# Another use of spare weight buffers, and a fourth seven-product pair in the last gate/up block

## The chip, the cores and the metric

The kernel runs on one core of one Trainium2 chip. The metric is the device time of one execution in microseconds (us). The median of three runs before the change is 1083.32 us (1082.24 to 1083.6).

PE is the matrix engine, DVE the vector engine, ACT the scalar engine, POOL the general-purpose engine, SP the engine that only issues transfers. "DMA" is a transfer between the chip's main memory and its on-chip memory.

## The reference

One decoder layer over 256 tokens with 2048 features, in float32. Cut to what matters here:

```python
u = rmsnorm(h, ln1_w[l])
proj = jnp.einsum('bsd,de->bse', u, w_in[l])
...                                   # recurrent heads and retention heads
y = jnp.concatenate([y_lru, y_ret], axis=-1)
h = h + jnp.einsum('bse,ed->bsd', y, w_out[l])
u = rmsnorm(h, ln2_w[l])
ff = jax.nn.silu(jnp.einsum('bsd,df->bsf', u, w_ffn_gate[l])) * jnp.einsum('bsd,df->bsf', u, w_ffn_up[l])
h = h + jnp.einsum('bsf,fd->bsd', ff, w_ffn_down[l])
return rmsnorm(h, final_norm_w)
```

The gate, up and down products (2048 by 5632, twice, and 5632 by 2048) are the largest part of the work.

## The kernel before, in words

**Precision.** A float32 matrix product is made of three passes in a faster format. Each operand is split into a high part (ACT rounds it, line 123) and a low part (DVE subtracts, line 124). `three` (lines 683 to 685) then issues high x high, high x low, low x high. So every weight tile that arrives must go through ACT and DVE before PE can use it.

**Blocks.** The output projection has two blocks (0, 1), gate/up eleven (2 to 12), down two (13, 14). A block makes two by two output tiles (c11, c12, c21, c22): two groups of 128 tokens by two groups of 512 weight columns. In a gate/up block one column group belongs to gate and the other to up. It sums over pairs of 128 features: eight pairs in blocks 0 to 12, 22 pairs in each block of down. A pair's weights are two raw tiles of 128 x 1024 (512 KB each), which are two column groups for two feature groups.

**Eight or seven products.** A pair is a 2 x 2 by 2 x 2 product of tiles. Done plainly it takes 8 products (`EIGHT`). A summed pair takes 7, by Strassen's method in Winograd's form: sums of the left tiles (s1 to s4) and of the weight tiles (t1 to t4, made by DVE in `add`, line 661) are multiplied in place of some of the tiles. In blocks 1 to 12 the seven products of a summed pair are done in two places. Four products (`share`) go to accumulators in the block *before*, and are combined there at the end of the shares (lines 805 to 811). Three products (`DIRECT`) are added in the block itself. For the share step both raw tiles are loaded, for the direct step the second one once more (class `Direct`, one load).

**Steps.** `SUMMED` names the summed pairs of each block, and `STEPS` the order of its work: p is a plain pair, s a share of the next block's summed pair, d a direct step of this block's, h half of a plain pair. Blocks 4 to 10 have four shares, four directs, and four plain pairs of which two are cut in halves. Block 12, the last of gate/up, shares three pairs for down (`EARLY_DOWN`). The left operands of those pairs (class `Left`: split, and for a summed pair four sums and another split) are made in block 12 too. The first block of down does its 22 pairs in the order `ORDER_DOWN`: 3, 4, 0, 5, 6, 1, 7, 8, 2, 9, and so on. Pairs 0, 1 and 2 are direct steps, 9, 12, 15, 17 and 19 are summed in place.

**Order.** The work is written out as a list of steps (`program`). A loop walks through it and issues the loads of the steps ahead by three raw tiles (`AHEAD`), then the step's products. All transfers of weights are issued by SP (lines 141, 641, 743, 771). A planner with a model of times then orders the instructions of each engine, gives out buffers, and puts in the waits; so the order on an engine is not exactly that of the list. Some work is deferred by a number of steps (`defer`, `tick`).

**Buffers.** Six raw tiles (`rpool`) and four pairs of split tiles (`wpool`). From block 3 on (`swap`) the space of the early stages gives two raw tiles and two pairs of split tiles more (`more`). Before the change a counter of all raw tiles sends every fourth load to an extra raw tile, and another counter every third split to an extra split tile. 60 tiles of 128 x 512 (`act_tile`) hold the activations, the left operands and some sums. `stop_more`, ahead of block 12, ends the use of the extra tiles. `swap_back`, ahead of down, gives their space to the residual rows, which lie in memory since the output projection and come back by POOL's queue (line 1112), and to the weights of the last norm (line 893).

Of the kernel before, what the change touches and what calls it, by code (L numbers as in the profile page):

```python
# [30 lines left out]

SUMMED = ((), (4, 5), (2, 3), (1, 2, 3)) + ((0, 1, 2, 3),) * 8 + ((1, 2, 3),)
SUMMED_OUT, SUMMED_FFN = (4, 5), (0, 1, 2, 3)

PLAIN = ((4, 5, 6, 7, 0, 1, 2, 3),) * 2 + (tuple(range(8)),) * 11
STEPS = ("pppspppspp", "ppspdpsdpp", "pdpsdpspspp", "pspsdpsdpsdp") + ("psdhsdhsdhsdhp",) * 7 + ("psdpsdpsddp", "psdpsdpsdpp")

# [7 lines left out]
def tile_hymba_layer(ctx: ExitStack, tc: tile.TileContext, A: dict, out: bass.AP):  # L45
# [5 lines left out]
    rpool = ctx.enter_context(tc.tile_pool(name="raw", bufs=6))  # L51
# [4 lines left out]
    tpool = early.enter_context(tc.tile_pool(name="tmp", bufs=6))  # L56
    late, resid, more, turn_of = [], [xpool], [], [0, 0]
    extra = ExitStack()
# [15 lines left out]
    def split_tiles():  # L74
        turn_of[1] += 1
        pool_ = more[1] if more and turn_of[1] % 3 == 0 else wpool
        return [pool_.tile([P, 1024], F32R, tag=g, name=nm(g)) for g in ("wh", "wl")]

    def raw_tile():
        turn_of[0] += 1  # L80
        pool_ = more[0] if more and turn_of[0] % 4 == 0 else rpool
        return pool_.tile([P, 1024], F32, tag="raw", name=nm("raw"))
# [76 lines left out]
    program = []  # L159
# [297 lines left out]
    half = {}  # L457
# [156 lines left out]
    NB = DFF // 512  # L614
    ff = [None] * (FT // 2)

    class Quad:
# [5 lines left out]
        def __init__(self, src, sums, before=None):  # L623
            self.src, self.sums, self.before = src, sums, before
            self.parts = {}
            self.apart = False

# [11 lines left out]
        def load(self, half):  # L639
            r = raw_tile()  # L640
            nc.sync.dma_start(out=r, in_=self.src[:, half * 1024 : half * 1024 + 1024])
            if half == 0 and self.before:
                self.before()
            if not self.sums:
                self.cut(("b22", "b21") if half else ("b11", "b12"), r)
                return
            if half == 0:
                self.ra = r
                self.parts["b11"] = act_tile("bh", F32R), act_tile("bl", F32R)
                split(*self.parts["b11"], r[:, :512])  # L650
                return
            self.cut(("b22", "b21"), r)
            self.add(r)
            self.cut(("t1", "t3"), self.ra)
            self.cut(("t2", "t4"), r)
# [31 lines left out]
    def block(index, quads, lefts, post, ps, tail, early={}, ordered=False):  # L687
# [39 lines left out]
        for i in range(n):  # L727
            program.append(([quads[i]], step(i)))

        def end():  # L730
# [29 lines left out]
    class Direct(Quad):  # L760
# [8 lines left out]
        def load(self, half):  # L769
            r = raw_tile()  # L770
            nc.sync.dma_start(out=r, in_=self.src[:, 1024:2048])
            self.cut(("b22", "b21"), r)
            self.parts["t4"] = self.shared.parts["t4"]
# [12 lines left out]
    class Block:  # L786
# [45 lines left out]
        def put(self, after):  # L832
            plain = [i for i in PLAIN[self.index] if i not in self.summed]
            for k, kind in enumerate(self.steps):
                if kind == "p":
                    i, n = plain.pop(0), len(plain)
                    quad = Quad(self.src(i), False)
                    run = lambda i=i, quad=quad, k=k, n=n: self.plain(i, quad, k == 0, n == 0)
                elif kind == "h":
# [266 lines left out]
    def swap_back():  # L1106
# [6 lines left out]
        load_fw()  # L1113

    blocks = [Block(d, lambda i, d=d: A["w_out"][8 * d + i], y, out_post(d), STEPS[d], SUMMED[d]) for d in range(2)]
    blocks += [
# [4 lines left out]
    for b, after in zip(blocks, blocks[1:] + [down]):  # L1121
        if b.index == 3:
            program.append(([], swap))
        if b.index == NB + 1:
            program.append(([], stop_more))
        b.put(after)
    program.append(([], swap_back))

# [119 lines left out]
```

## Time and profile before

| what | value |
|---|---|
| median of three runs | 1083.32 us |
| the profiled execution, its own time | 1082.46 us |
| its span, first to last instruction | 1080.7 us |
| granted clock of the matrix engine, mean | 0.998 |
| PE busy, share of the span | 1070.2 us, 99% |
| DVE busy | 964.1 us, 89% |
| ACT busy | 664.5 us, 61% |
| raw tiles loaded for gate/up, 512 KB each | 216 |
| raw tiles loaded for down, 512 KB each | 91 |

The page splits the span into 40 slices and gives the busy share of each engine in tenths. The chain that ended last is followed from the last instruction back to what released it. Groups of instructions carry the line of the kernel, the engine, the tile written and the tiles read (`c<-wl,ah` is a matmul into an accumulator c from a low weight part and a high activation part), the count, the busy time and the mean. In views in order of time the first number is the start and the second the duration, both in us.

### The profile page before, as it was taken

To read this page: it belongs to the slowest core of one execution; us is meant where nothing else is said; L and a number is where in the kernel's file an instruction comes from. 1 tells how busy PE (TensorE), PEld (TensorE's weight loads), DVE (VectorE), ACT (ScalarE), POOL (GpSimd) and SP (SyncE) were. 2 spreads that over 40 slices of the span, in tenths; PEclk is the share of its full clock that TensorE was granted. 3 is DMA by queue.
4 is the path that set the end of the run, shared out by engine and by line. 5 is a ranking of instruction groups with operands and counts; after the bars stand their busy time and mean duration, and the time that the engine had idled before them with its cause. 6 is when DMAs were issued, how large, how long until landed. Compare 5 with 4: busy or idle time off the path is not lost.

```text
span 1080.7 us, 14590 instructions
## 1 busy us (share of the span) xinstructions
PE 1070.2 (99%) x5089; PEld 897.7 (83%) x5089; DVE 964.1 (89%) x1399; ACT 664.5 (61%) x947; POOL 57.2 (5%) x73
## 2 busy tenths in 40 slices
PE   9999999999999999999999999999999999999997
PEld 7888888888888888888888888888888888888886
DVE  7889789988878889989999999999999889997886
ACT  7666644468756676656656565665656656654563
POOL 0602230000000000000000000000002000000001
PEclk9999999999999999999999999999999999999999
DMA  9965475554556588677776777777767856474662
GB/s 325 336 213 171 159 254 166 183 176 158 192 195 234 183 304 273 231 235 256 257 270 228 251 260 242 263 269 232 258 234 270 289 181 214 162 245 159 214 212 101
DMA packets 71386, 244.62 MB, mean 226 GB/s; under 512 B 8208, under 2 KB 8592, under 8 KB 71312
## 3 DMA queue, kind: packets, MB, share of 16 engines
q1 hardware_dynamic: 68400, 236.34, 64.6%
q0 software_dynamic: 1472, 4.72, 1.3%
q10 hardware_dynamic: 1440, 2.62, 0.6%
q8 instruction: 40, 0.66, 0.2%
q14 instruction: 34, 0.28, 0.1%
HBM read 239.46 MB, written 4.19 MB: 225 GB/s over the span
## 4 chain that ended last, share of the span: by engine, by line
PE 98%; DVE 1%; DMA 1%; POOL 0%; SPq 0%; ACT 0%; issue 0%; POOLq 0%; ACTq 0%
PE c L685 22%; PE c L683 22%; PE c L684 22%; PE fm L194 11%; PE fm L196 5%; PE tm L174 3%; PE tm L175 3%; PE tm L176 3%; PE p L683 1%; PE p L685 1%; PE p L684 1%; PE ft L865 1%; DMA x<-in_x 1%; PE ht L588 0%; PE sc L492 0%; DVE wl L124 0%
## 5 line engine op out<-in xcount | busy, mean ns | idle before, releaser
L123 ACT CAST wh<-raw 128x1024 fp32r<-128x1024 f32 (+1 forms) x498 | 462.9, 959 | 323.8 <-PE c L685 130.8
L124 DVE TENSOR_TENSOR wl<-raw,wh 128x1024 fp32r<-128x1024 f32 (+1 forms) x498 | 542.2, 1115 | 72.5 <-ACT wh L123 71.2
L684 PE MATMUL c<-wl,ah 128*128 128x512 f32 x826 | 322.7, 391 | 0.0
L685 PE MATMUL c<-wh,al 128*128 128x512 f32 x826 | 321.8, 390 | 0.0
L683 PE MATMUL c<-wh,ah 128*128 128x512 f32 x826 | 280.3, 391 | 0.0
L683 PEld LDWEIGHTS c<-wh,ah 128*128 128x128 f32 x826 | 155.1, 188 | 32.0 <-ACT wh L123 0.3
L685 PEld LDWEIGHTS c<-wh,al 128*128 128x128 f32 x826 | 155.2, 188 | 31.8
L684 PEld LDWEIGHTS c<-wl,ah 128*128 128x128 f32 x826 | 155.2, 188 | 31.6
L194 PE MATMUL fm<-u,wh 128*128 128x512 f32 x512 | 161.4, 396 | 0.0
L196 PEld LDWEIGHTS fm<-u,wl 128*128 128x128 f32 x512 | 96.1, 188 | 22.4
L196 PE MATMUL fm<-u,wl 128*128 128x256 f32 x512 | 101.2, 279 | 0.0
L661 DVE TENSOR_TENSOR raw<-raw,raw 128x512 f32<-128x512 f32 x114 | 78.4, 689 | 2.0
L661 DVE TENSOR_TENSOR raw<-raw 128x512 f32<-128x512 f32 x114 | 78.3, 688 | 1.4
L194 PEld LDWEIGHTS fm<-u,wh 128*128 128x128 f32 x512 | 78.4, 189 | 0.3
L684 PE MATMUL c<-wl,sh 128*128 128x512 f32 x192 | 74.3, 390 | 0.0
L685 PE MATMUL c<-wh,sl 128*128 128x512 f32 x192 | 73.7, 390 | 0.0
L683 PE MATMUL c<-wh,sh 128*128 128x512 f32 x192 | 67.3, 391 | 0.3 <-ACT sh L123 0.3
L176 PE MATMUL tm<-wh,u 128*128 128x512 f32 x128 | 48.7, 391 | 0.0
L175 PE MATMUL tm<-wl,u 128*128 128x512 f32 x128 | 48.7, 393 | 0.0
L174 PE MATMUL tm<-wh,u 128*128 128x512 f32 x128 | 46.9, 394 | 1.4 <-ACT u L298 1.4
L683 PEld LDWEIGHTS c<-wh,sh 128*128 128x128 f32 x192 | 36.1, 188 | 8.1 <-ACT sh L123 0.7
L685 PEld LDWEIGHTS c<-wh,sl 128*128 128x128 f32 x192 | 36.1, 188 | 7.5
(247 smaller groups left out, 1027.4 us busy)
## 6 DMA issues: line engine op xcount, KB each, us to landing
raw<-in_w_gu SPq DMA_DIRECT2D x216, 512.0 KB, 5.3
raw<-in_w_down SPq DMA_DIRECT2D x91, 512.0 KB, 4.6
raw<-in_w_out SPq DMA_DIRECT2D x34, 512.0 KB, 3.7
raw<-in_w_lx SPq DMA_DIRECT2D x16, 512.0 KB, 6.4
raw<-in_w_k SPq DMA_DIRECT2D x16, 512.0 KB, 3.6
raw<-in_w_q SPq DMA_DIRECT2D x16, 512.0 KB, 4.2
raw<-in_w_rg SPq DMA_DIRECT2D x16, 512.0 KB, 3.5
raw<-in_w_lg SPq DMA_DIRECT2D x16, 512.0 KB, 3.5
```

The costliest lines, as they stand in the source:

```text
L123: act.copy(out=dst_h, in_=src)
L124: v.tensor_tensor(out=dst_l, in0=src, in1=dst_h.bitcast(F32), op=ALU.subtract)
L174: pe.matmul(ps, ah, wh, start=first, stop=False)
L175: pe.matmul(ps, ah, wl, start=False, stop=False)
L176: pe.matmul(ps, al, wh, start=False, stop=last)
L194: pe.matmul(ps, wh, hl, start=n + i == 0, stop=False)
L196: pe.matmul(ps[:, :S], wl, hl[:, :S], start=False, stop=n + i == len(order) - 1)
L661: v.tensor_tensor(out=dst, in0=a, in1=b, op=ALU.add)
L683: pe.matmul(p, ah, bh, start=first, stop=False, skip_group_check=onto)
L684: pe.matmul(p, ah, bl, start=False, stop=False, skip_group_check=onto)
L685: pe.matmul(p, al, bh, start=False, stop=last, skip_group_check=onto)
L865: pe.transpose(pt[:, o : o + P], g[:, (2 * b + c) * P : (2 * b + c) * P + P], ident)
```

## The change

- Block 12's summed pairs become (0, 1, 2, 3) instead of (1, 2, 3). So block 11 shares four pairs, with the steps that blocks 4 to 10 have, and block 12 takes the steps that block 11 had.
- The extra raw tiles no longer go to every fourth load. They go to the load of each direct step, and to the second load of a block's last plain pair (`brief`).
- The counter of splits stays (every third).
- `stop_more` moves from the start of block 12 to behind the tenth step of the first block of down (position 9, pair 9). `swap_back`, with the residual rows' return, moves from the start of down to behind its thirteenth step (position 12, pair 12).

```diff
-SUMMED = ((), (4, 5), (2, 3), (1, 2, 3)) + ((0, 1, 2, 3),) * 8 + ((1, 2, 3),)
+SUMMED = ((), (4, 5), (2, 3), (1, 2, 3)) + ((0, 1, 2, 3),) * 9
...
-STEPS = ("pppspppspp", "ppspdpsdpp", "pdpsdpspspp", "pspsdpsdpsdp") + ("psdhsdhsdhsdhp",) * 7 + ("psdpsdpsddp", "psdpsdpsdpp")
+STEPS = ("pppspppspp", "ppspdpsdpp", "pdpsdpspspp", "pspsdpsdpsdp") + ("psdhsdhsdhsdhp",) * 8 + ("psdpsdpsddp",)
...
     def split_tiles():
-        turn_of[1] += 1
-        pool_ = more[1] if more and turn_of[1] % 3 == 0 else wpool
+        turn_of[0] += 1
+        pool_ = more[1] if more and turn_of[0] % 3 == 0 else wpool
...
-    def raw_tile():
-        turn_of[0] += 1
-        pool_ = more[0] if more and turn_of[0] % 4 == 0 else rpool
+    def raw_tile(brief=False):
+        pool_ = more[0] if more and brief else rpool
...
         def load(self, half):
-            r = raw_tile()
+            r = raw_tile(self.brief and half == 1)
...
         for i in range(n):
             program.append(([quads[i]], step(i)))
+            if i in hooks[ordered]:
+                program.append(([], hooks[ordered][i]))
...
     class Direct(Quad):
...
         def load(self, half):
-            r = raw_tile()
+            r = raw_tile(True)
...
                     quad = Quad(self.src(i), False)
+                    quad.brief = n == 0
...
+    hooks = {0: {9: stop_more, 12: swap_back}, 1: {}}
...
         if b.index == 3:
             program.append(([], swap))
-        if b.index == NB + 1:
-            program.append(([], stop_more))
         b.put(after)
-    program.append(([], swap_back))
```

More of the change, by code (lines that the diff above doesn't have):

```diff
@@ L56, in tile_hymba_layer @@
     tpool = early.enter_context(tc.tile_pool(name="tmp", bufs=6))
-    late, resid, more, turn_of = [], [xpool], [], [0, 0]
+    late, resid, more, turn_of = [], [xpool], [], [0]
     extra = ExitStack()
@@ L625, in __init__ @@
             self.parts = {}
-            self.apart = False
+            self.apart = self.brief = False
         def cut(self, names, raw):
```

## The prediction

> **What bounds the kernel now.** I read the page first, then PE's waits, then PE's order of time, then the stretches of the blocks that the change touches.
>
> ```profile
> span 1080.7 us, 14590 instructions
> ...
> PE 1070.2 (99%) x5089; PEld 897.7 (83%) x5089; DVE 964.1 (89%) x1399; ACT 664.5 (61%) x947; POOL 57.2 (5%) x73
> ...
> PEclk9999999999999999999999999999999999999999
> ...
> PE 98%; DVE 1%; DMA 1%; POOL 0%; SPq 0%; ACT 0%; issue 0%; POOLq 0%; ACTq 0%
> ...
> L123 ACT CAST wh<-raw 128x1024 fp32r<-128x1024 f32 (+1 forms) x498 | 462.9, 959 | 323.8 <-PE c L685 130.8
> ```
>
> PE is on 98% of the chain that ended last, at full clock in every slice; DVE is next, busy 89%. A busy PE can still run below its pace, so the next two views matter more. The first is everything that PE waited for, in the whole span (us in total, times, longest); the second is PE's order of time where the last gate/up block begins.
>
> ```profile
> PE tm L174 <- ACT u L298: 1.4, 2, 1.0
> PE warm L116 <- DVE eps_t L109: 1.1, 1, 1.1
> PE c L683 <- ACT sh L123: 0.3, 1, 0.3
> ```
>
> ```profile
> 812.37 0.39 PE L683 MATMUL c<-wh,ah 128*128 128x512 f32 x1
> 812.60 0.39 PE L684 MATMUL c<-wl,ah 128*128 128x512 f32 x1
> 812.82 0.39 PE L685 MATMUL c<-wh,al 128*128 128x512 f32 x1
> 813.05 0.39 PE L683 MATMUL c<-wh,ah 128*128 128x512 f32 x1
> ```
>
> PE waited 2.8 us in all, and none of it in the gate/up blocks from the second on or in down: the two larger waits are at the start, and the third, 0.3 us, is on the path in an output-projection block. Starts follow each other by (813.05 - 812.37) / 3 = **0.227 us** for one matmul of 512 columns. So this kernel is a count of matmuls times 0.227 us over almost its whole length. There is no stall in the changed stretch that more buffers could remove; they can only prevent one.
>
> **The change part by part.**
>
> *The products.* Each product is three matmuls. A plain pair has 8 products (24 matmuls); a summed pair has 4 in the share step and 3 in the direct step (12 + 9 = 21). Pair 0 of the last gate/up block goes from plain to summed. In the block before it, the steps become those of the eight blocks with four shares and four directs: 12 matmuls more there. In the last block a plain pair goes (-24) and a direct step comes (+9). Net 12 - 24 + 9 = **-3 matmuls, 3 x 0.227 = -0.68 us**. The name of the change says four such pairs, but three of them are there already; only one is new.
>
> *What the new pair costs off PE.* One weight tile more is loaded (512 KB), and DVE and ACT split and add more. The prices are DVE's starts in a stretch where it runs without a gap:
>
> ```profile
> 892.52 1.22 DVE L124 TENSOR_TENSOR wl<-raw,wh 128x1024 fp32r<-128x1024 f32 x1
> 893.65 0.68 DVE L124 TENSOR_TENSOR bl<-raw,bh 128x512 fp32r<-128x512 f32 x1
> 894.25 1.22 DVE L124 TENSOR_TENSOR wl<-raw,wh 128x1024 fp32r<-128x1024 f32 x1
> 895.39 0.69 DVE L124 TENSOR_TENSOR al<-ff,ah 128x512 fp32r<-128x512 f32 x1
> 895.99 0.29 DVE L561 TENSOR_TENSOR s<-ff 128x128 f32<-128x128 f32 x1
> 896.19 0.28 DVE L563 TENSOR_TENSOR s<-ff 128x128 f32<-128x128 f32 x1
> ```
>
> From start to start a split of 1024 columns takes 1.13 us, one of 512 takes 0.60, a 128-column operation 0.20; an addition of 512 columns is taken like the split of its size. A share step has four additions and three splits of 512, and one split of 1024: 7 x 0.60 + 1.13 = 5.33 us. A direct step has 1.13, a plain pair 2.26. The left operand of a summed pair of down, made in the last block, has 2 x 0.60 + 4 x 0.20 = 2.0. A block's combining and gating, six operations of 512 columns, is about 3.7.
>
> - The block before the last: 4 plain + 3 shares + 4 directs + 3.7 = 33.3 us before; one share more makes 38.6.
> - The last block: 5 plain + 3 shares + 3 directs + 3.7 + 3 x 2.0 = 40.4 before; 39.2 after (one plain pair less, one direct more).
>
> PE in the same two blocks: 351 matmuls before and 348 after, and 16 transposes.
>
> ```profile
> 857.22 0.66 PE ft L865 x6
> ```
>
> At 0.66 / 6 = 0.11 us each these add 1.8 us: 81.4 us before, 80.7 after. So DVE's spare time falls from 81.4 - 73.7 = 7.7 us to 80.7 - 77.8 = **2.9 us** over two blocks, and in the last block alone it is 168 x 0.227 + 0.9 = 39.0 us of PE against 39.2 us of DVE. What hides this work today can be seen in the stretches from one block's transposes to the next (a steady block, the last but one, the last) and in down; after the length stand the busy us of PE, of its weight loads, of DVE, ACT and POOL, then clock, DMA share and GB/s:
>
> ```profile
> 735.20:775.50 40.30, 40.30 (x184) 33.42 (x182) 38.28 (x49) 25.84 (x34) 0.00 (x0) 1.00 0.74 248
> 775.50:816.40 40.90, 40.90 (x188) 33.94 (x186) 37.41 (x51) 24.95 (x34) 2.17 (x4) 1.00 0.68 224
> 816.40:856.50 40.10, 40.10 (x183) 33.23 (x182) 36.17 (x50) 24.86 (x34) 4.23 (x8) 1.00 0.89 316
> ...
> 891.00:930.00 39.00, 39.00 (x174) 32.31 (x173) 38.29 (x58) 25.73 (x32) 0.00 (x0) 1.00 0.59 201
> ```
>
> The steady blocks already run with DVE at 38.3 of 40.3 us, and a stretch of down with 38.3 of 39.0, and PE waits in neither. The last but one becomes a steady block. The last has no spare of its own and must live on its lead. That there is a lead shows in what ACT waits for in these blocks:
>
> ```profile
> ACT wh L123 <- PE c L685: 20.8, 15, 3.8
> ...
> ACT wh L123 <- DMA raw<-in_w_gu: 1.1, 3, 0.5
> ```
>
> ACT, which begins each split, waits 20.8 us for PE to free a split buffer, and 1.1 us for data: the splitting is as far ahead as its buffers allow. I cost the added DVE work at nothing. If the cover were gone, the two blocks would take DVE's 77.8 us and about 2 us of gaps in each (40.30 - 38.28), 81.8 us against PE's 80.7: a loss of 1.1 us.
>
> *The extra raw buffers.* Before, every fourth load takes one. Counting loads, 96 go to the projections and 58 to the first three blocks that follow; with the 21 of the next, the steady blocks of 20 loads each begin on load 176, a multiple of four. Their loads 4, 8, 12 and 16, counted from 0, are exactly the four direct steps. So the new rule does there what the count does already, but for one of five: the last pair's second half takes the place of the first pair's first half. It changes the second gate/up block, the last two, and down. Worth between nothing and the longest wait for a weight split that PE shows, 0.3 us, either way; I take 0.
>
> *The later end of the extra buffers and the refill that moves.* The residual rows (eight transfers of 256 KB) and the norm's weights (four) come into the space of the extra buffers, on POOL's queue. Here are that refill, its first use, and the first product of down's first summed pair (its tenth step, after which the extra buffers are given up):
>
> ```profile
> L1112 POOL DMA_DIRECT2D htok<-kept_rows x8: 536/536/538, 824.9 to 828.6; - x8
> ...
> L920 DVE TENSOR_TENSOR htok<-htok,part x8: 682/688/691, 949.1 to 1059.7; 128x512 f32<-128x512 f32 x8
> ...
> DMA to landing us min/median/max: 2.3/5.4/11.2
> ```
>
> ```profile
> L683 PE MATMUL p<-bh,ah x12: 389/389/390, 890.4 to 1039.3; 128*128 128x512 f32 x12
> ```
>
> Loads run three tiles ahead, so the last extra split buffer belongs to step 12, which ends 21 + 24 + 24 matmuls after 890.4, at 906.0. Issue takes 8 x 0.54 = 4.3 us, landing at most 11.2: by 922 at the latest, and the rows are wanted at 949.1. Cost 0, with 27 us to spare. POOL has no other work there, so nothing queues behind its wait.
>
> A page of the skill speaks against this move: the Trainium skill, "SBUF — State Buffer", section "SBUF: two separate sides", says that a transfer issued from GpSimd's queue starves for descriptors while VectorE, in some of its modes, holds the port that they share. The trace does not show it: the refills landed in at most 11.2 us beside a DVE that was busy 36.17 of 40.10 us. By the page the refill could be late at 949; by the row the sum stays.
>
> *Sum.* 1082.46 us for the profiled execution (1080.7 span, 1.8 around it) less 0.68 is 1081.8. The profiled execution lies 0.86 below the median of the runs, 1083.32, so for a median I forecast **1082.64, say 1082.6**.
>
> **The rivals.**
>
> *Room for the left operands runs out (slower).* The activation pool has 60 tiles. As the last block begins, after the change, there live 24 tiles of the eight left operands, 20 of the product of gate and up or their precursors, and 8 (before: 6) of the shared pairs' last sums: 52. The first share takes 5 net, the next wants 5 more at once: 62. It fits only when the first plain pair is over and frees two. If I miscounted by two, it waits until the first direct step is over, 45 matmuls or 10.2 us into the block; then left operand, share and one cast (0.96, the mean on the page) take about 2.0 + 5.3 + 1.0 = 8.3 us, to 18.5, and PE wants it after 69 matmuls, at 15.6: a stall of 2.9 us, or 1083.3 - 0.7 + 2.9 = 1085.5. Against it: nothing before shows PE waiting for such a tile, and the planner may put other matmuls there. It decides from a lead of under 8.3 us on.
>
> *DVE becomes the bound in the last two blocks.* Worked out above: -0.7 + 1.1, or 1083.7. For it the 2.9 us left of 80.7; against it the steady blocks at the same load.
>
> *The refill collides with the weights.* Two stretches, the old refill and where it goes:
>
> ```profile
> raw<-in_w_gu SPq DMA_DIRECT2D x5, 512.0 KB, 9.2
> htok<-kept_rows POOLq DMA_DIRECT2D x8, 256.0 KB, 8.1
> ```
>
> ```profile
> raw<-in_w_down SPq DMA_DIRECT2D x15, 512.0 KB, 4.6
> ```
>
> Beside the refill a weight tile lands after 9.2 us instead of 4.6. In down that delay meets a DVE with 0.7 us of spare in 39. If it passed to PE once, it would cost 4.6 us: 1087.2. Against it: at the old place it made ACT wait 1.1 us and PE not at all. A refill that is itself late at 949.1 needs 43 us from 906, where the slowest before took 4.3 + 11.2; I give that under 0.01, inside this rival. The Trainium skill, "DMA: Bandwidth & Descriptors", section "Issuing engines are not separate DMA queues", says that transfers from different queues interleave on the same 16 engines; the 9.2 us agrees with it.
>
> *The order moves elsewhere.* A planner orders all instructions by a modelled time, so the new buffers can shift PE's order from the second gate/up block on. One stall or one less of the 0.3 us kind: 1082.3 to 1082.9, not told from the forecast.
>
> *The change does not do what it says*, if the added matmuls equalled the removed ones: 1083.3. The counts exclude it.
>
> **How the numbers follow.** A measurement of this kernel tells about 0.2% (2.2 us) from no change: below 1081.15 is faster, above 1085.49 slower. Chances: forecast, the last two rivals with it, 0.77; DVE as the bound 0.09; room for left operands 0.06; refill collision 0.04; a loss spread over several of these, or a gain I see no source for, 0.04. Faster 0.04 (only 0.68 us is in sight, and runs differ by 1.4), slower 0.09 (half of the room rival, the refill, half of the spread loss), no change 0.87. The range goes from the lowest run less the gain and one spared stall (1082.24 - 0.68 - 0.3 = 1081.3) up to where the DVE rival with the same spread of the runs still fits and the room rival begins, 1085.0.
>
> **What would show it.** Right: three PE matmuls fewer; starts 0.227 us apart through both blocks; PE's waits after 400 us still none; the last matmul some 0.7 us earlier; refill issued near 906 and landed before 925. Wrong: a PE wait for a share's split or a left operand between 812 and 835 (room, or DVE), weight tiles landing late and a PE gap at 915 to 930 (refill), or a PE wait in an earlier block (order).

## The result and the profile after

The changed kernel takes 1089.76 us (median of four runs, 1089.27 to 1090.21). The kernel before, run on the same chip beside it, takes 1083.46 us (1082.24 to 1083.9). The ratio is 1.0060, 95% interval 1.0042 to 1.0077: **6.3 us slower**, where 1082.6 was forecast and 1085.0 was the upper end of the range.

First the rows of the page of the changed kernel that answer to those of before. The profiled execution took 1090.02 us.

```profile
span 1088.2 us, 14581 instructions
...
PE 1074.2 (99%) x5086; PEld 897.5 (82%) x5086; DVE 968.6 (89%) x1406; ACT 666.4 (61%) x950; POOL 56.6 (5%) x73
```

PE has 5089 - 5086 = 3 matmuls fewer, as worked out. DVE has 968.6 - 964.1 = 4.5 us more to do. Yet the span is 1088.2 - 1080.7 = 7.5 us longer. The busy shares, 99 and 89%, are the same as before and say nothing of it. The two longest of what PE waited for, in the whole span of the changed kernel (total, times, longest), do:

```profile
PE c L682 <- ACT ah L122: 2.4, 1, 2.4
PE c L682 <- ACT c L810: 1.4, 1, 1.4
```

Both are new. Each occurred once, the first for the cast of a left operand (`ah`), the second for a copy in the combining of a share (line 810). PE's order of time in the changed kernel shows where (start, duration, and in brackets the wait and its releaser):

```profile
850.58 0.84 PE L684 MATMUL c<-wh,sl 128*128 128x512 f32 x3
853.79 0.50 PE L682 MATMUL c<-wh,ah 128*128 128x512 f32 x1 [2.38 <-ACT ah L122]
854.13 0.40 PE L683 MATMUL c<-wl,ah 128*128 128x512 f32 x1
855.96 0.80 PE L682 MATMUL c<-wh,ah 128*128 128x512 f32 x1 [1.44 <-ACT c L810]
856.55 0.63 PE L683 MATMUL c<-wl,ah 128*128 128x512 f32 x1
856.98 1.05 PE L684 MATMUL c<-wh,al 128*128 128x512 f32 x2
857.83 0.63 PE L682 MATMUL c<-wh,ah 128*128 128x512 f32 x1
858.26 0.63 PE L683 MATMUL c<-wl,ah 128*128 128x512 f32 x1
858.69 0.63 PE L684 MATMUL c<-wh,al 128*128 128x512 f32 x1
859.11 0.48 PE L682 MATMUL c<-wh,ah 128*128 128x512 f32 x1
859.43 0.40 PE L683 MATMUL c<-wl,ah 128*128 128x512 f32 x1
```

This is where gate/up ends and down begins. From 850.58 to 859.43 there are 13 steps from start to start. At 0.227 us they would take 2.95 us; they took 8.85, so **5.9 us are lost here**. The two waits are 3.8 of it. Another part comes after them: from 856.55 to 859.11 the starts are 2.56 / 6 = 0.427 us apart in place of 0.227, which costs 1.2 us. The rest, 0.9 us, is the slow first starts behind each wait. Outside this stretch the changed kernel lost 0.8 us near 595, some 0.6 between 825 and 850, and 0.5 each near 1006 and 1017; elsewhere the pace is that of before.

Why were the operands late? Take two DVE instructions that both kernels have and that close a chain: the gating of the last block but one, and the last addition with which the last block's shares are combined. In the kernel before:

```profile
813.20 1.40 DVE L876 SCALAR_TENSOR_TENSOR gated<-c,r_tok,gated 128x512 f32<-128x512 f32 x2
...
847.58 0.70 DVE L811 TENSOR_TENSOR c<-c,p 128x512 f32<-128x512 f32 x1
```

And in the changed kernel:

```profile
820.74 1.40 DVE L878 SCALAR_TENSOR_TENSOR gated<-c,r_tok,gated 128x512 f32<-128x512 f32 x2
...
857.18 0.69 DVE L812 TENSOR_TENSOR c<-c,p 128x512 f32<-128x512 f32 x1
```

DVE comes to the first 7.5 us later and to the second 9.6 us later. ACT's part of the same combining moved too. Its rows in the kernel before, and then in the changed one:

```profile
837.97 0.57 ACT L806 COPY p<-c 128x512 f32<-128x512 f32 x1
...
846.42 0.58 ACT L809 COPY c<-q 128x512 f32<-128x512 f32 x1
```

```profile
850.39 0.57 ACT L807 COPY p<-c 128x512 f32<-128x512 f32 x1
...
853.12 1.14 ACT L122 CAST ah<-ff 128x512 fp32r<-128x512 f32 x2
...
855.32 0.59 ACT L810 COPY c<-q 128x512 f32<-128x512 f32 x1
```

Before, the first of the shares' accumulators was copied out at 838, and PE had other matmuls for the 8.5 us until the combining's last copy began. After, the copy begins at 850.39, when PE is at its last share products; behind them stand only products that need the left operand (cast at 853.12) and the combined sums (855.32 + 0.59 = 855.9). What PE waits for is made while nothing covers it.

The refill went where the prediction had put it:

```profile
904.84 4.23 POOL L1114 DMA_DIRECT2D htok<-kept_rows  x8 [17.89 <-PE c L684]
```

Two theories follow. **Work**: DVE's added work in the last two gate/up blocks uses up the lead with which operands are ready. **Order**: the extra split tiles that now last into down let the plain pairs go ahead, so that the last share ends at the block's end. The rivals of the prediction (room for left operands, the refill) stay to be tested.

### The profile page after: what moved, and what is told of

Read it like the earlier page. It is cut to its first block, busy times and chain, and to the rows that moved or that the text cites. A ratio compares the mean times of both kernels' runs of the same rounds, so it can differ in the third digit from the quotient of the medians.

```text
span 1088.2 us, 14581 instructions
## 1 busy us (share of the span) xinstructions
PE 1074.2 (99%) x5086; PEld 897.5 (82%) x5086; DVE 968.6 (89%) x1406; ACT 666.4 (61%) x950; POOL 56.6 (5%) x73
## 5 line engine op out<-in xcount | busy, mean ns | idle before, releaser
L684 PE MATMUL c<-wh,al 128*128 128x512 f32 x820 | 318.4, 390 | 0.0
```

What stands on the lines that cost most here:

```text
L684: pe.matmul(p, al, bh, start=False, stop=last, skip_group_check=onto)
```

## The experiments

Each time is given against that of the kernel before, run on the same chip beside it. The kernel's loss is in the difference, and the interval is that of the ratio.

### The two halves of the change

The products alone: the kernel before with only this edit.

```diff
-SUMMED = ((), (4, 5), (2, 3), (1, 2, 3)) + ((0, 1, 2, 3),) * 8 + ((1, 2, 3),)
+SUMMED = ((), (4, 5), (2, 3), (1, 2, 3)) + ((0, 1, 2, 3),) * 9
-STEPS = (...) + ("psdhsdhsdhsdhp",) * 7 + ("psdpsdpsddp", "psdpsdpsdpp")
+STEPS = (...) + ("psdhsdhsdhsdhp",) * 8 + ("psdpsdpsddp",)
```

> Only the new products: block 12 sums four pairs, steps as in the change; extra buffers by the old count, given up ahead of block 12, refill ahead of down. Theory COVER: the loss after the change comes from down's first products waiting for the combining of the last share; in PE's written order 37 matmuls lie between that share and down's own first product before, 1 after the change, 21 here. The combining took about 5.5 us after the change (850.4 to 855.9), 21 matmuls are 4.8 us, so a stall of at most 1 us: 1083.0 to 1084.5. Theory DVE BOUND: the added splits are what costs, and they are all here: 1088 to 1090, with PE waiting for splits. Theory ROOM (60 activation tiles): the two more tiles of sums are here too, so 1086 to 1090.

Measured: 1084.77 against 1082.96 us, ratio 1.0018 (1.0009 to 1.0028).

The buffers alone: the changed kernel with the two lines above as they were before.

> Only the buffers: block 12 sums three pairs as before; extra raw tiles by the new rule, extra buffers kept to the tenth step of down, refill behind the thirteenth. COVER: 18 matmuls between the last share and down's own first product, 4.1 us against 5.5: a stall of 1 to 2 us, and more if PE's clock drops after it: 1084 to 1086. DVE BOUND and ROOM: no added work, no added tiles, so as before, 1083.3. If the late refill were the cause: 1088 to 1090 with the loss near 905 us.

Measured: 1083.25 against 1082.96 us, ratio 1.0002 (0.9993 to 1.0011).

So the buffers cost nothing by themselves, the products lose 1.8 us, and both together 6.3. What PE waited for in the products alone is at the same place, at 850 to 853, but smaller:

```profile
PE c L683 <- ACT ah L123: 1.0, 1, 1.0
PE c L685 <- DVE al L124: 0.6, 1, 0.6
```

The traced execution took 1086.71 us, 1.9 above the median. Behind its two waits come 3.41 us at half clock, which a traced execution of the same order further below (1085.25 us) does not have. So it shows where the loss is, and not how much of the 1.8 us is there.

The same two DVE instructions in the products alone:

```profile
817.11 1.41 DVE L876 SCALAR_TENSOR_TENSOR gated<-c,r_tok,gated 128x512 f32<-128x512 f32 x2
...
853.18 0.69 DVE L811 TENSOR_TENSOR c<-c,p 128x512 f32<-128x512 f32 x1
```

They are 3.9 and 5.6 us later than before the change. The prediction had 5.3 us more DVE work in the last block but one; it is paid from the lead there, and not won back in the last block.

### Which of the extra buffers

The changed kernel with the extra split tiles given up ahead of block 12, the raw ones as in the change:

```diff
-        pool_ = more[1] if more and turn_of[0] % 3 == 0 else wpool
+        pool_ = more[1] if len(more) > 1 and turn_of[0] % 3 == 0 else wpool
...
+        if b.index == NB + 1:
+            program.append(([], more.pop))
```

> The change, but the extra split tiles are given up ahead of block 12 as before; extra raw tiles and refill as in the change. COVER: the extra split tiles let the splits of plain pairs go ahead of the last share's; without them 21 matmuls lie between, as with the products alone: 1083.0 to 1084.5, no stall above 1 us at the start of down. DVE BOUND, ROOM or the moved refill: still 1088 to 1090, since work, tiles and refill are those of the change.

Measured: 1085.81 against 1082.96 us, ratio 1.0026 (1.0016 to 1.0035). This takes back 3.4 of the 6.3 us.

The reverse, raw tiles given up early and split tiles kept late:

```diff
+    raw_off = []
...
-        pool_ = more[0] if more and brief else rpool
+        pool_ = more[0] if more and brief and not raw_off else rpool
...
+        if b.index == NB + 1:
+            program.append(([], lambda: raw_off.append(1)))
```

> The change, but the extra raw tiles are given up ahead of the last gate/up block, as before the change; only the extra split tiles last into down. The products alone gave 1084.8 us, the products with the raw tiles late and the split tiles early 1085.8, the whole change 1089.8. Theory SPLIT TILES: with split tiles to spare, the plain pairs are split and multiplied ahead of the last share, so that the share ends right ahead of down and its combining has no matmuls beside it. Then this kernel is as slow as the whole change, 1089 to 1090.5, with the two waits (for a left operand's cast and for the combining's copy) near 851 to 856. Rival RAW TILES: it is the raw tiles that last; then it comes out like the products alone, 1084.3 to 1085.8, with at most 1 us of wait ahead of down.

Measured: 1092.1 against 1083.76 us, ratio 1.0083 (1.0066 to 1.0100): as slow as the whole change and 2 us more. PE's order of time in this kernel:

```profile
852.47 0.84 PE L685 MATMUL c<-wh,sl 128*128 128x512 f32 x3
856.81 0.79 PE L683 MATMUL c<-wh,ah 128*128 128x512 f32 x1 [3.50 <-ACT ah L123]
```

Again the last share's products (`sh`, `sl`) stand directly ahead of the first that needs a left operand. It is the late split tiles that bring the larger loss. The late raw tiles move it by 1 to 2 us, up where the split tiles end early (2.9 against 1.8) and down where they last (6.3 against 8.3). The program's own order says the same of the split tiles: down's first product outside the shares is the 37th matmul behind the last product of a share before the change, the 18th with the buffers alone, and the 21st with the products alone or with the split tiles given up early. Where products and late split tiles come together, with the change and in this kernel, it is the very next one.

### Is it the room for left operands?

The changed kernel with two activation tiles more, paid for with one raw tile:

```diff
-    apool = ctx.enter_context(tc.tile_pool(name="acts", bufs=60))
-    rpool = ctx.enter_context(tc.tile_pool(name="raw", bufs=6))
+    apool = ctx.enter_context(tc.tile_pool(name="acts", bufs=62))
+    rpool = ctx.enter_context(tc.tile_pool(name="raw", bufs=5))
```

> The change with 62 activation tiles in place of 60, paid for with one raw tile (5 in place of 6). ROOM: the stall at the start of down goes, 1082.5 to 1084.5. COVER: PE's order at that place is unchanged (1 matmul between), so the loss stays: 1088 to 1091, a little worse where the missing raw tile is felt.

Measured: 1098.84 against 1082.96 us, ratio 1.0148 (1.0131 to 1.0165). The wait for the left operand is there as before, and longer:

```profile
PE c L682 <- ACT ah L122: 3.1, 1, 3.1
```

Two tiles more did not take the wait away. The changed kernel's own trace speaks against room too: ACT makes two weight casts from 851.23 on, 1.99 us long, and goes straight on to the cast of the left operand at 853.12, so that this cast stood behind others in ACT's order and did not wait for a free tile. The other 9 us of this run are likely the lost raw tile's, which was not tried alone.

### Are the shares in the wrong place?

The order of block 12 with its shares earlier, with the products alone and with the whole change:

```diff
-STEPS = (...) + ("psdhsdhsdhsdhp",) * 8 + ("psdpsdpsddp",)
+STEPS = (...) + ("psdhsdhsdhsdhp",) * 8 + ("psdsdsdpdpp",)
```

> Products alone (as the first run of this study), with the steps of block 12 in the order psdsdsdpdpp in place of psdpsdpsddp: the same steps, shares and directs first, two plain pairs last. PLACE: DVE catches up in the plain pairs, 55 matmuls between the last share and down's own first product: no stall, 1082.0 to 1083.3. WORK: the sum of work is the same, so 1084 to 1086.

> The change as it is, with the same new order of block 12's steps. PLACE: 46 matmuls between in place of 1: no stall at the start of down, 1082.5 to 1084.5 with the smaller waits elsewhere (0.6 near 594, 0.9 after 1000). WORK: 1088 to 1090.

Measured: 1091.37 against 1083.75 us (1.0070; 1.0053 to 1.0087) and 1089.55 us (1.0050; 1.0035 to 1.0065). There is no wait left ahead of down. In the first of the two PE waits inside block 12 instead, at 826 to 837:

```profile
PE c L684 <- DVE wl L124: 2.2, 2, 1.6
PE c L683 <- ACT wh L123: 1.4, 2, 0.9
```

Moving the shares moves the loss. A better order of the same work is not enough, at least not this one; the work itself has to be tested.

### DVE's work by itself

First, idle DVE work in the kernel before, nine operations of 512 columns in block 11 or in block 12, with no other edit (12 instead of 11 for the second):

```diff
             self.add(r)
+            if self.more_dve:
+                for _ in range(3):
+                    v.tensor_tensor(out=sumsq, in0=sumsq, in1=sumsq, op=ALU.max)
```

> The kernel before, with three idle vector operations of 128x512 more in each of the three shares of block 11 (9 x 0.60 = 5.4 us of DVE, what the added share costs there); PE's order and all tiles as before. Theory WORK (DVE has too much to do for the PE time of the last two blocks): spare falls from 7.7 to 2.3 us over the two blocks, less than after the change (2.9), so a stall at the start of down like that of the products alone: 1085 to 1088. Theory PLACE (what costs is that the last share now stands closer to the end of its block, with a direct step in place of a plain pair behind it, so that DVE has no light steps to catch up in before down begins): order and steps are those of before, so nothing: 1082.5 to 1084.0.

> The same 9 operations, 5.4 us, in the three shares of block 12. WORK: the block has 42.4 us of PE and then 45.8 us of DVE: 3.4 us or more at the start of down, and a drop of the clock after it: 1086 to 1090. PLACE: the two plain pairs at the end give DVE 6.4 us to catch up, so under 1 us: 1083 to 1084.5.

Measured: 1083.40 and 1083.39 against 1083.75 us (0.9996 and 0.9995). Both tell nothing. Nothing in the program depended on these operations, so the planner put them where DVE was idle. The instruction view of the second has their first and last start:

```profile
L756 DVE TENSOR_TENSOR sumsq<-sumsq x9: 662/677/693, 46.4 to 61.7; 128x512 f32<-128x512 f32 x9
```

The second attempt holds them in place: they work on a share's raw tile, between its additions and its casts (each takes the maximum of a tile with itself, so that the data stay).

```diff
             self.add(r)
+            if self.more_dve:
+                for _ in range(3):
+                    v.tensor_tensor(out=r[:, :512], in0=r[:, :512], in1=r[:, :512], op=ALU.max)
...
+            for sh in self.shared:
+                sh.more_dve = index == NB + 1
```

> The kernel before with the same 9 idle vector operations (5.4 us) as in the fifth run, now on the share's own raw tile between its additions and its splits, so that they stay in block 11. WORK: the block has 38.7 us of DVE in 39.4 of PE, so it just fits: 1083.0 to 1084.5, a stall under 1 us at most. ORDER (only the planned place of the last share and the extra split tiles count): 1083.0 to 1084.0.

> The same 9 operations (5.4 us) held in the shares of block 12. WORK: 45.8 us of DVE in 42.4 of PE, 3.4 us too much and about 2 us of gaps: a stall of 3 to 6 us at the start of down and a drop of the clock behind it: 1086 to 1090. The planner now puts 2 matmuls between the last share and down's own first product in place of 37, as after the change. If the work were harmless: 1083 to 1084.

Measured: 1089.13 against 1083.32 us (1.0054; 1.0039 to 1.0069) and 1089.47 us (1.0056; 1.0039 to 1.0073). So 9 x 0.60 = 5.4 us of DVE work, with no product changed, costs 6 us. In block 11, where theory WORK had expected that it just fits, PE waits 2.0 us for a copy of the combining and 1.2 us for a weight cast, at 809 to 814. With the work in block 12, PE waits for what it waits for in the changed kernel:

```profile
PE c L683 <- ACT ah L123: 2.4, 1, 2.4
```

Two things keep this pair from showing DVE's load alone. The held operations also lengthen each share's own chain, by 3 x 0.60 = 1.8 us, as leaving out additions, below, shortens it; load and chain are not parted. And with the work in block 12 the planner changed PE's order as well: down's first product became the 2nd matmul behind the last share's, where it was the 37th.

Now the other direction: the products alone and the whole change, each without the 12 additions of block 12's three shares (7.2 us of DVE; the weight sums are then not made, and the products that use them take other data).

```diff
-            self.add(r)
+            if not self.no_add:
+                self.add(r)
...
+            for sh in self.shared:
+                sh.no_add = index == NB + 2
```

> Products alone, without the four additions in each of the three shares of block 12 (left out, 12 x 0.60 = 7.2 us of DVE less; pairs 0 to 2 of down are then computed from wrong sums). WORK: 32 us of DVE in 39.0 of PE: no stall at the start of down, the three matmuls show: 1082.0 to 1083.5. If the place of the shares alone counts: still 1084 to 1086.

> The whole change without the same additions (left out, 7.2 us of DVE less; pairs 0 to 2 of down are computed from wrong sums). WORK: nearly all of the loss goes, 1082.5 to 1084.5; what is left are the small waits elsewhere (0.6 near 594, 0.9 after 1000). If the extra split tiles cost by themselves, through the order in which casts stand in ACT's queue: 12 matmuls between, 2.7 us against some 5 us of combining, so 1085 to 1088.

Measured: 1082.59 against 1083.32 us (0.9991; 0.9981 to 1.0000) and 1084.74 us (1.0011; 1.0002 to 1.0021). The products alone now show no wait of PE in gate/up and down, and the time lies 0.73 us lower. That agrees with the 0.68 us of the three matmuls, but the interval reaches 1.0000. With the late split tiles 2.15 us more remain, with one wait of 1.3 us for a left operand's low part: less work shrinks the loss of the order and does not end it. The order moved with the work in these two as well: down's first product is the 28th behind the last share's in the first (21st with the additions) and the 12th in the second (the next one with them).

### How much of it, and where

One share less, the last of the three, in the products alone (4 x 0.60 = 2.4 us of DVE; that share's products take other data):

```diff
+                sh.no_add = index == NB + 2 and sh is self.shared[2]
```

> The products alone, with the four additions of one of the three shares of the last gate/up block left out (4 x 0.60 = 2.4 us less on DVE; its weight sums are then not made, and the products that use them take other data). A dose between the products alone (1084.77 us, 0 left out) and all twelve additions left out (1082.59 us, 7.2 us left out). Theory WORK: the loss goes with the work, so 1083 to 1084.3. Rival THRESHOLD ELSEWHERE (it was the missing of all additions, a shorter share, that mattered): no less than 1084.5.

Measured: 1083.16 against 1083.76 us, ratio 0.9997 (0.9988 to 1.0007). The loss of 1.8 us is gone, and down's first product is the 25th behind the last share's, close to the 21st of the products alone. In the rows of this kernel the combining's last addition begins 4.0 us sooner than in the products alone (849.20 against 853.18):

```profile
849.20 0.69 DVE L814 TENSOR_TENSOR c<-c,p 128x512 f32<-128x512 f32 x1
```

Can the work be moved rather than left out? POOL is idle there. The 12 small sums of down's left operands go to POOL, in the products alone:

```diff
-        def __init__(self, f, sums):
+        def __init__(self, f, sums, e=v):
...
-                v.tensor_tensor(out=s1, in0=a22, in1=a21, op=ALU.subtract)
+                e.tensor_tensor(out=s1, in0=a22, in1=a21, op=ALU.subtract)
...
-            dl[p] = Left(ff[p], p in EARLY_DOWN + SUMMED_DOWN[0] + SUMMED_DOWN[1])
+            dl[p] = Left(ff[p], p in EARLY_DOWN + SUMMED_DOWN[0] + SUMMED_DOWN[1], pool if p in EARLY_DOWN else v)
```

> The products alone, with the 12 sums of 128 x 128 for the left operands of down's first three summed pairs made on POOL: DVE has 12 x 0.20 = 2.4 us less to do in the last gate/up block, nothing is left out. Theory WORK (DVE's load in the last gate/up block is what costs): the 1.6 us of waits that the products alone show ahead of down shrink or go, 1082.7 to 1084.0. Rival SHARED MEMORY PATH: POOL's work slows DVE beside it by as much as it takes off, 1084.5 or more.

Measured: 1084.61 against 1083.76 us, ratio 1.0015 (1.0006 to 1.0024).

The same, and one share's four additions on POOL as well (`self.on` is POOL for the second share):

```diff
-                v.tensor_tensor(out=dst, in0=a, in1=b, op=ALU.add)
+                self.on.tensor_tensor(out=dst, in0=a, in1=b, op=ALU.add)
```

> The products alone, with the left sums of down's first summed pairs and the four weight additions of one share on POOL; nothing is left out. DVE has 4.8 us less to do in the last gate/up block, but POOL takes 1.7 us for an addition of 512 columns where DVE takes 0.60, so that this share's additions last some 7 us instead of 2.4. Theory WORK: 1082.3 to 1083.5, the three matmuls' 0.7 us showing. Rival LATENCY: POOL's slower additions make this share late: a wait for a share's cast or low part of 1 us or more, and 1084.5 or more.

Measured: 1087.82 against 1083.76 us, ratio 1.0042 (1.0027 to 1.0057). POOL is too slow for it, and it slows DVE. DVE's row for one group of splits in the products alone, its row for the same group in this kernel, and a row of POOL in this kernel:

```profile
828.51 4.09 DVE L124 TENSOR_TENSOR wl<-raw,wh 128x1024 fp32r<-128x1024 f32 x4
```

```profile
828.87 6.17 DVE L124 TENSOR_TENSOR wl<-raw,wh 128x1024 fp32r<-128x1024 f32 x4 [0.57 <-ACT wh L123]
```

```profile
829.53 2.15 POOL L663 TENSOR_TENSOR raw<-raw 128x512 f32<-128x512 f32 x1
```

The group is three splits of 1024 columns and one of 512, though the row carries the first one's shape. It takes 4.09 us alone and 6.17 beside POOL, and one addition on POOL takes 2.15 us where DVE needs 0.60. The 1.54 us in the second expectation below is 6.17 / 4 and takes the four for equal; single splits of 1024 columns took 1.47 to 2.31 us here.

Last, the refill. In the run with the sums on POOL, POOL's queue holds the refill at 816 to 820 ahead of the sums. So its return was written behind the thirteenth step of down, for the products alone and for the products with the sums on POOL:

```diff
+            if i in hooks[ordered]:
+                program.append(([], hooks[ordered][i]))
...
+    hooks = {0: {12: swap_back}, 1: {}}
...
-    program.append(([], swap_back))
```

> The products alone, with the return of the residual rows and the norm's weights moved behind the thirteenth step of the first block of down, as the change moves it; the extra raw and split tiles stay given up ahead of the last gate/up block, so the order of the work is that of the products alone. In the products alone the rows return between 820 and 831, and ACT then waits 0.9, 1.6 and 1.0 us for three weight tiles of down near 845 to 849, just ahead of the two waits of PE. Theory TRANSFERS: those late tiles are part of the loss; with the refill gone from there the waits of PE shrink, 1082.5 to 1084.0 against 1084.8. Theory WORK ALONE: the tiles would have been split no earlier, DVE being full; no difference to the products alone, 1084.3 to 1085.3.

> The left operands' 12 sums on POOL and the late return of the residual rows together, with the products; nothing is left out. With the sums on POOL alone the time was 1084.61; there POOL's queue stands in the wait for its refill from 810.7 to 816.0 and issues it until 820.3, and the sums come behind it. Theory QUEUE: with the refill gone the sums come up to 9 us sooner and the weights land sooner, so the loss is gone and the three matmuls' 0.7 us show: 1082.3 to 1083.5. Rival: POOL beside DVE lengthens DVE's instructions (from 1.13 to 1.54 us for a split of 1024 columns in the run with a share's additions on POOL), so that nothing is won over the late refill without POOL's sums.

Measured: 1084.84 against 1082.93 us (1.0015; 1.0006 to 1.0024) and 1084.26 us (1.0014; 1.0005 to 1.0023). The edit did not do what it was to do: the planner issues the refill as soon as its space is free, and the space was still given up ahead of block 12. POOL's row in the first of the two:

```profile
816.96 4.22 POOL L1114 DMA_DIRECT2D htok<-kept_rows  x8 [5.83 <-PE c L685]
```

So neither run tests the refill, and they serve as repetitions of the products alone (1084.77) and of the sums on POOL (1084.61). Their traces still tell why moving 2.4 us off DVE helped so little. DVE's rows with the sums on POOL:

```profile
822.63 0.75 DVE L124 TENSOR_TENSOR al<-ff,ah 128x512 fp32r<-128x512 f32 x1 [1.48 <-ACT ah L123]
824.50 0.69 DVE L124 TENSOR_TENSOR wl<-raw,wh 128x512 fp32r<-128x512 f32 x1 [1.12 <-ACT wh L123]
...
853.20 0.69 DVE L813 TENSOR_TENSOR c<-c,p 128x512 f32<-128x512 f32 x1
```

Rid of those sums, DVE stood idle 2.6 us ahead of these two instructions for ACT, which in turn was waiting for PE; in the products alone it is 1.5 us. The combining's last addition begins at 853.20, as in the products alone (853.18). In the run without the last share's additions the 2.4 us came off later, at 836 to 840, and the addition began at 849.20. So the place at which DVE is relieved counted, not only the amount.

A second cause may stand ahead of down. What ACT waited for between 800 and 860 in the products alone has this row:

```profile
ACT wh L123 <- DMA raw<-in_w_down: 3.4, 3, 1.6
```

Weight tiles of down landed late there, by 3.4 us in sum. In the run with the sums on POOL and the refill's edit it is 3.2, in the other run with that edit, which has the program order of the products alone, 1.1, and PE's two waits follow: 1.0 + 0.6, 1.07 + 0.61 and 0.63 + 0.62 us. In the run without the last share's additions ACT waits for no tile of down up to 850. A raw tile is free for the next load only when its splits are done, so a late DVE makes a late load; how much of the loss of the products is DVE's own lateness and how much these landings', the runs do not part, and it stays open.

No version here is faster than the kernel before by more than a measurement tells. A version with the three matmuls saved and nothing left out was not found.

## Why the prediction was wrong, step by step

- **Three matmuls, -0.68 us: right.** 5086 against 5089; where the loss is removed (the products without additions) the time falls by 0.73 us, at the edge of what the runs tell from nothing.
- **The raw tiles' rule, 0: right with the buffers alone**, 1.0002. Together with the new products, giving up the raw tiles late or early moves the time by 1 to 2 us, for which no term stood.
- **The refill near 906, landed in time, cost 0: right.** It is issued at 904.84, its transfers land within 7.6 us, and PE waits for nothing there. The rival of a collision with the weights falls with it.
- **"I cost the added DVE work at nothing": the first step that failed.** The working had 2.9 us to spare over two blocks and noted that the last block lives on its lead. It then priced the lost cover as a rival of 1.1 us with a chance of 0.09. The products alone show it: 1.8 us over before, and with the 0.7 us that were saved, 2.5 us lost. The mechanism was the rival's; its size was missed by more than half. The sum over the block let work and spare time trade places freely, but the shares' combining and the left operands come last in the block, so the lateness (3.9 us at the gating, 5.6 at the combining) falls on the few instructions that PE needs first in down. And in the changed kernel 3.4 us at half clock followed the waits, worth 1.2 us, which no term held. The lead itself was read from ACT's waits for PE, 20.8 us, as splitting that "is as far ahead as its buffers allow". The same view of the kernel before holds another row, which speaks against that: ACT waited 13.1 us for the shares' additions on DVE.

```profile
ACT wh L123 <- DVE raw L661: 13.1, 5, 3.7
```

- **"There is no stall in the changed stretch that more buffers could remove; they can only prevent one": the second, and the larger.** More split tiles made one. The term for the later end of the extra buffers counted the refill alone, "Cost 0", and nothing for the order that the split tiles allow. The order rival had named the way ("the new buffers can shift PE's order"), but priced it by the longest wait seen, 0.3 us. It costs 6.3 - 1.8 = 4.5 us on top of the products, and the two runs with one kind of extra tile each put that on the split tiles: with the raw tiles late, keeping the split tiles costs 6.3 - 2.9 = 3.4 us, and with the raw tiles early 8.3 - 1.8 = 6.5. With the buffers alone the same tiles cost nothing.
- **Room for left operands: fell.** Two tiles more left the wait in place.
- **What would show it wrong** named a wait for a left operand or a share's split "between 812 and 835". The kind was right; the place was 851 to 856, one block boundary later.

By what was measured the sum reads -0.7 for the matmuls, +2.5 for the added work and +4.5 for the order. The last term is the remainder of the 6.3; its own two measurements, 3.4 and 6.5, stand on either side of it.

## What to carry to other kernels

DVE, busy some 95% of a block here (38.3 of 40.3 us), had a lead to spend rather than spare time, so an added cost is to be looked for at the next place where short chains must end in time and not in the block's average. Buffers that are free by themselves can change the order that a planner chooses, and an order that finishes the independent work first leaves a chain's end bare; count the matmuls that stand between the chain's last input and its first use. Work that is added as a probe has to be tied into the data flow, or it drifts to where it costs nothing.

## What the runs showed of the hardware

**Whether a wait brings the slower clock depends on where it falls.** The two runs with the refill written late have the same two waits ahead of down, with two different lengths. The first, the products alone:

```profile
851.57 0.50 PE L683 MATMUL c<-wh,ah 128*128 128x512 f32 x1 [0.63 <-ACT ah L123]
...
852.91 0.50 PE L685 MATMUL c<-wh,al 128*128 128x512 f32 x1 [0.62 <-DVE al L124]
853.25 0.40 PE L683 MATMUL c<-wh,ah 128*128 128x512 f32 x1
853.49 0.39 PE L684 MATMUL c<-wl,ah 128*128 128x512 f32 x1
```

And the second, with the sums on POOL:

```profile
851.39 0.50 PE L683 MATMUL c<-wh,ah 128*128 128x512 f32 x1 [1.07 <-ACT ah L123]
...
852.74 0.53 PE L685 MATMUL c<-wh,al 128*128 128x512 f32 x1 [0.61 <-DVE al L124]
...
853.91 0.63 PE L685 MATMUL c<-wh,al 128*128 128x512 f32 x1
854.34 0.63 PE L683 MATMUL c<-wh,ah 128*128 128x512 f32 x1
```

After 0.63 + 0.62 us of waiting PE goes on at 0.24 us from start to start; after 1.07 + 0.61 it takes 0.43 us for the next 3 us. In the changed kernel the granted clock (the column behind POOL's) is 1.00 while PE waits and 0.50 in the 3.4 us behind:

```profile
852.48:855.88 3.40, 0.73 (x2) 0.30 (x2) 3.40 (x5) 3.40 (x6) 0.00 (x0) 1.00 0.96 345
855.90:859.30 3.40, 3.34 (x8) 2.67 (x9) 3.28 (x6) 0.01 (x1) 0.00 (x0) 0.50 0.87 347
```

But the length of the waits does not decide it. The kernel with the work held in block 12 has the longer waits of 2.38 and 0.85 us at the same place, and keeps the full clock. Its first wait, and its clock in the stretch behind:

```profile
854.92 0.50 PE L683 MATMUL c<-wh,ah 128*128 128x512 f32 x1 [2.38 <-ACT ah L123]
```

```profile
853.48:856.90 3.42, 1.98 (x8) 1.34 (x8) 3.42 (x5) 3.42 (x6) 0.00 (x0) 1.00 0.78 287
```

The clock records of the traces tell the two apart. Nine of the twenty traces hold a stretch at half clock between 300 and 1060 us, and it lasts 3.41 or 6.83 us. The stretches at full clock before and behind it are whole numbers of 3.413 us: in the changed kernel 849.92 and 225.28 us, 249 and 66 of them. So the clock of these runs changes only at the edges of windows of 3.41 us that lie end to end, and what counts is how long PE is idle within one window. Between 300 and 1060 us, a window with up to 1.58 us of idle time was never followed by a drop. One with 1.62 us or more was, at its end, with one exception at 1.68 us (the run with two more activation tiles). The busy times of PE are modelled, so this limit, near half a window, is an estimate. In the changed kernel PE was idle for 2.68 us of one window. The 2.38 us wait above lies across an edge, and leaves 0.93 us in one window and 1.44 in the next. The ten times of the products alone, 1083.94 to 1086.71 us, would fit executions with and without such a drop, but only the one of 1086.71 us was traced.

The Trainium skill, "TensorE: Matmul & The Clock Gate", section "Part 1: The HAM clock gate (the "warmup" mystery)", tells of a clock that falls to half after an idle window of about 3.4 us and is released after as much activity. The half rate and the length of some 3.4 us agree. A window idle throughout is not needed here: 1.62 us of one was enough.

**POOL and DVE take turns.** Beside POOL the group of four splits took 6.17 us in place of 4.09. Two of the instructions that overlap, DVE's first and then POOL's:

```profile
830.46 2.31 DVE L124 TENSOR_TENSOR wl<-raw,wh 128x1024 fp32r<-128x1024 f32 x1
```

```profile
831.64 1.44 POOL L561 TENSOR_TENSOR s<-ff 128x128 f32<-128x128 f32 x1
```

The addition on POOL shown further above (829.53, 2.15 us) ends at 831.68. DVE's split ends at 832.77, 1.09 us later, about the 1.13 us that a split takes alone. POOL's small sum, in turn, ends at 833.08, 0.31 us behind DVE's split. So each seems to have done its work only when the other was through, and its time in the trace holds that wait. The Trainium skill, "SBUF — State Buffer", section "SBUF: two separate sides", tells of a port that the two share, which one instruction holds for its whole length while the other fully blocks. The rows agree with it.
